# Cross-attention in a one-core float32 encoder block: a third pair of k-tiles in seven products, and the softmax's transposes queued behind the newest unit

## The chip, the cores and the metric

The kernel runs on one core of a Trainium2 chip. The metric is the time of one execution on the device in microseconds (us), and a lower time is better. A core has TensorE (PE in the profile, with its weight loads as PEld), VectorE (DVE), ScalarE (ACT), GpSimd (POOL) and SyncE (SP, which issues the loads here). Every engine takes the instructions of its own queue in the order in which they stand there, and waits on semaphores for results of the others.

## The reference

One encoder layer over 256 tokens of width 2048, in float32. The change lies in the cross-attention with 256 memory tokens and 4 heads of width 512:

```python
def mem_cross_attention(h, mem_h, w_q, w_kv, w_o):
    q = (h @ w_q).reshape(b, s, XATTN_HEADS, XATTN_HEAD_DIM)
    kv = (mem_h @ w_kv).reshape(b, mem_h.shape[1], 2, XATTN_HEADS, XATTN_HEAD_DIM)
    k, v = kv[:, :, 0], kv[:, :, 1]
    logits = jnp.einsum('bshd,bmhd->bhsm', q, k).astype(jnp.float32) * (XATTN_HEAD_DIM ** -0.5)
    p = jax.nn.softmax(logits, axis=-1).astype(v.dtype)
    o = jnp.einsum('bhsm,bmhd->bshd', p, v).reshape(b, s, D_MODEL)
    return o @ w_o
...
    x = x + 0.5 * swiglu(rms_norm(x, ffn1_norm[l]), ...)
    x = x + mixer(rms_norm(x, mix_norm[l])) @ w_out[l]
    x = x + mem_cross_attention(rms_norm(x, xattn_norm[l]), rms_norm(mem, mem_norm[l]), ...)
    x = x + 0.5 * swiglu(rms_norm(x, ffn2_norm[l]), ...)
return rms_norm(x, final_norm)
```

## The kernel before

**Splitting.** Each float32 operand is split in two parts of the matmul type `fp32r`: a high part (a cast on ScalarE) and a low part (source minus high part, on VectorE). One product a·w is three matmuls: high·high, high·low, low·high. The activations of the keys' and values' stage stand split in `xs`; the weights are split as they arrive.

**Units.** All weights come in units of 1 MB (`raw`, three buffers). For a projection in `block_s` a unit holds one pair of k-tiles (2 × 128 rows) for 1024 output columns; a block has eight units, pairs 0 to 7 in a given order, and its result is 256 tokens × 1024 columns. The class `Stream` collects units and other steps (`st.unit`, `st.op(f, after)`: f comes `after` units later) and issues them in that order. The split of a unit stands two units ahead of its products (`AHEAD`), and the split halves have three buffers (`wh`, `wl`). A plain unit (`unit_p`) takes eight products, 24 matmuls of 512 columns. Its split is one cast and one subtraction over 2048 columns.

**Seven products.** A pair that is listed in a `Sums` object is taken with seven products instead of eight (the 2×2 scheme of Strassen and Winograd), 21 matmuls (`seven`, line 507). For it VectorE makes sums of the four weight blocks (`split_seven`, line 486: one over 1024 columns, two over 512), and two parts are split: the sums (`wh`, `wl`) and three of the four raw blocks (`xh`, `xl`, lines 279 and 280). The activations' sums are made once for each pair (`Sums.make`). In the keys' and values' stage `xh` and `xl` share one tag of two buffers (`att`).

**PSUM.** `ptile` hands out four tiles of two banks each, and these four are all of PSUM. A block holds two of them for its result from its first unit to its last (`open_whole`). From its first pair of seven products to its last it holds the two others for the products that are shared among the blocks (`open_parts`). `combine` (lines 574 to 579) reads those two out into an SBUF tile `sg`, and `join` (line 589) adds the first two to it.

**Keys and values.** Two rounds, b = 0 and 1: a block for the keys of heads 2b and 2b+1, then a block for the values of these heads, then (after the second round) the output projection `w_o`. Steps that belong to the keys are placed among the units of the values' block that follows: `turn_K` (transposes of the keys, 1 unit later), `logits` (line 1319: 24 matmuls of 256 columns for each head, then maximum, scaling, exponential, reciprocal and scaling on VectorE and ScalarE), `probs` (line 1341: four transposes of the probabilities and their split `PT`, 3 units later). `values` (line 1358) comes one unit after the values' block. Each of these takes PSUM tiles from the same four. K and V of a head share two buffers (`kv`), so the split of V waits for the logits that read K.

**Order.** The list of `Stream` is the program's order. Then a scheduler places the instructions on the engines' queues: it may put an instruction ahead of earlier ones that can't be issued yet. `in_turn`, `among_weights` and `tc.issue_after` fix an order: the instruction stands behind the named one on its queue. `latest` keeps the last weight instruction of ScalarE and VectorE for it.

Of the kernel before, what the change touches and what calls it, by code (L numbers as in the profile page):

```python
# [14 lines left out]
P = 128  # L15
D = 2048
# [4 lines left out]
NB = 512  # L21
# [78 lines left out]
def build(ctx, tc, I, out):  # L100
    nc = tc.nc
    st = Stream()
# [34 lines left out]
    def ptile(name):  # L137
        return psum.tile([P, 2, NB], F32, tag="ps", name=name)
# [6 lines left out]
    def uid(s):  # L145
        cnt[0] += 1
        return f"{s}{cnt[0]}"
# [25 lines left out]
    ident = head.tile([P, P], F32, tag="ident", name="ident")  # L173
# [16 lines left out]
    xs = main.tile([P, KT, 2, S], F32R, tag="xs", name="xs")  # L190
# [64 lines left out]
    latest = {}  # L255
# [14 lines left out]
    def among_weights(f):  # L270


        scalar, vector = behind_weights(f)
        latest["vector"] = vector
        if scalar is not None:
            latest["scalar"] = scalar
# [7 lines left out]
    def split(hi, lo, src):  # L284
        high = nc.scalar.copy(hi, src)
        return high, nc.vector.tensor_tensor(out=lo, in0=src, in1=f32(hi), op=ALU.subtract)
# [70 lines left out]
    def products(ps, act, k, h, wh, wl, first, last):  # L357

        tok = slice(h * P, (h + 1) * P)
        parts = [(act[:, k, 0, tok], wh), (act[:, k, 0, tok], wl), (act[:, k, 1, tok], wh)]  # L360
        for i, (a, w) in enumerate(parts):
            nc.tensor.matmul(ps, a, w, start=first and i == 0, stop=last and i == 2)  # L362

    def block_t(srcs, act, evict, delays=(0, 0), amid=None):

# [127 lines left out]
    def seven(banks, act, sums, g, fresh, ends, weights, order):  # L493
        th, tl, rh, rl = weights
        k0, k1, lo, hi = 2 * g, 2 * g + 1, slice(0, P), slice(P, S)
        a11, a12, a22 = ([act[:, k, p, t] for p in range(2)] for k, t in ((k0, lo), (k1, lo), (k1, hi)))
        s3, n1, n4, s2 = sums.parts(g)
        table = {
            "P1": (a11, rh[:, 0], rl[:, 0]), "P3": (n4, rh[:, 1], rl[:, 1]),
            "P2": (a12, rh[:, 2], rl[:, 2]), "P5": (n1, th[:, 0], tl[:, 0]),  # L500
            "P7": (s3, th[:, 1], tl[:, 1]), "P6": (s2, th[:, 2], tl[:, 2]),
            "P4": (a22, th[:, 3], tl[:, 3]),
        }
        for n in order:
            (a, b), wh, wl = table[n]
            for j, (x, w) in enumerate(((a, wh), (a, wl), (b, wh))):
                nc.tensor.matmul(  # L507
                    banks[n], x, w, start=n in fresh and j == 0, stop=n in ends and j == 2
                )

# [115 lines left out]
    def wload(dst, w, k0, n, n0, cols=NB):  # L626
        nc.sync.dma_start(
            dst, w[k0 * P : (k0 + n) * P, n0 : n0 + cols].rearrange("(k p) n -> p k n", p=P)
        )
# [9 lines left out]
    def wwide(w, n0, k0=0, nk=KT):  # L639

        def src(k):
            def load(raw):
                raw = raw.rearrange("p (k n) -> p k n", n=2 * NB)
                if len(loaded) < 3:
                    for kk in range(2):
                        parts = (0, NB) if not loaded else (0,)
                        for c in parts:
                            n = 2 * NB // len(parts)
                            wload(raw[:, kk : kk + 1, c : c + n], w, k + kk, 1, n0 + c, n)
                else:  # L650
                    wload(raw, w, k, 2, n0, 2 * NB)
                next(first_loads, None)
                loaded.append(1)
            return load
        return [src(k0 + k) for k in range(0, nk, 2)]
# [557 lines left out]
    for b in range(2):  # L1213
        block_b(wblock(w_in, (4 + b) * NB), xs, ev_v(b))
        for i in range(2):
            h = 2 * b + i
# [16 lines left out]
    def homes(of):  # L1233
        return lambda: scope.update(shared={tag: list(of[tag]) for tag in of})
# [5 lines left out]
    xa = {}  # L1240

    def xt(name, shape, dt=F32, tag=None, bufs=1):
        t = whole_lines(scope["pool"], shape, dt, tag or name, uid(name), bufs)
        xa[name] = t
        return t
# [36 lines left out]
    w_q, w_kv, w_o = I["xattn_w_q"][0], I["xattn_w_kv"][0], I["xattn_w_o"][0]  # L1282
# [2 lines left out]
    q_sums, Q_ORDER = Sums("ye", xs, (4, 5), True, 2), ((0, 1, 2, 3, 6, 4, 5, 7),  # L1285
                                                        (0, 1, 4, 2, 5, 3, 6, 7))
    Q_SEVENS = ((4,), (4, 5))
    kv_sums, KV_ORDER = Sums("ye", xs, (0, 4), True, 2), (1, 5, 2, 0, 3, 6, 4, 7)
    held = {}

    def ev_Q(b):
# [10 lines left out]
    def turn_K(h):  # L1302
        v = rows_turned(held["K", h])
        K = xa["K", h] = xt("K", [P, 4, 2, M], F32R, tag="kv", bufs=2)
        split(K[:, :, 0, :], K[:, :, 1, :], v)

    def ev_V(b):
        def evict(j, c):
            V = xa["V", 2 * b + j] = xt("V", [P, 2, 2, XHD], F32R, tag="kv", bufs=2)
            split(V[:, :, 0, :], V[:, :, 1, :], c)  # L1310
        return evict

    def logits(h):
        ps = ptile(uid("pl"))
        for t in range(2):
            tok = slice(t * P, (t + 1) * P)
            parts = [(d, a, b) for d in range(4) for a, b in ((0, 0), (0, 1), (1, 0))]
            for i, (d, a, b) in enumerate(parts):
                nc.tensor.matmul(  # L1319
                    ps[:, t, :M], ys[:, 4 * h + d, a, tok], xa["K", h][:, d, b, :],  # L1320
                    start=i == 0, stop=i == 11,
                )
        scale = XHD ** -0.5
        nm, sm = xt("nm", [P, 2], bufs=2), xt("sm", [P, 2], bufs=2)
        nc.vector.tensor_reduce(out=nm, in_=ps[:, :, :M], axis=AX.X, op=ALU.max)
        nc.vector.tensor_scalar_mul(nm, nm, -scale)
        pr = xa["P", h] = xt("P", [P, 2, M], bufs=2)
        for t in range(2):
            nc.scalar.activation(
                pr[:, t, :], ps[:, t, :M], AF.Exp, scale=scale, bias=nm[:, t : t + 1],  # L1330
                accum_out=sm[:, t : t + 1],
            )
        nc.vector.reciprocal(out=sm, in_=sm)
        for t in range(2):
            nc.vector.tensor_scalar_mul(pr[:, t, :], pr[:, t, :], sm[:, t : t + 1])

    def probs(h):
        ps = ptile(uid("pt"))
        for mtile in range(2):
            for t in range(2):  # L1340
                nc.tensor.transpose(
                    ps[:, mtile, t * P : (t + 1) * P], xa["P", h][:, t, mtile * P : (mtile + 1) * P], ident
                )
        if h % 2 == 0:
            xt("PT", [P, D], F32R)
        PT = xa["PT", h] = xa["PT"][:, h % 2 * 4 * S : (h % 2 + 1) * 4 * S].rearrange(
            "p (m a s) -> p m a s", m=2, a=2
        )
        split(PT[:, :, 0, :], PT[:, :, 1, :], ps[:, :, :S])

    def values(h):
        for p in range(2):
            ps = ptile(uid("pv"))
            for d in range(2):
                col = slice((2 * p + d) * P, (2 * p + d + 1) * P)
                parts = [(m, a, b) for m in range(2) for a, b in ((0, 0), (0, 1), (1, 0))]
                for i, (m, a, b) in enumerate(parts):
                    nc.tensor.matmul(  # L1358
                        ps[:, d, :S], xa["V", h][:, m, a, col], xa["PT", h][:, m, b, :],
                        start=i == 0, stop=i == 5,  # L1360
                    )
            split_pair(ys, 4 * h + 2 * p, ps[:, :, :S])
# [8 lines left out]
            for c, after in enumerate((5, 7, 6, 9)):  # L1371
                st.op(lambda c=c: mem_fold(c), after)
    st.op(homes(KV_HOMES))
    for g, after in zip(kv_sums.pairs, (0, 2)):
        st.op(lambda g=g: among_weights(lambda: kv_sums.make(g)), after)
    for b in range(2):
        block_s(wwide(w_kv, b * 2 * NB), xs, kv_sums, KV_ORDER, lambda j, c, b=b: held.__setitem__(
            ("K", 2 * b + j), c))
        for j in (1, 0):
            h = 2 * b + j  # L1380
            st.op(lambda h=h: turn_K(h), 1)
        for h in (2 * b, 2 * b + 1):
            st.op(lambda h=h: logits(h), 2)
            st.op(lambda h=h: probs(h), 3)
        block_s(wwide(w_kv, D + b * 2 * NB), xs, kv_sums, KV_ORDER, ev_V(b))
        for h in (2 * b, 2 * b + 1):
            st.op(lambda h=h: values(h), 1)
    st.op(homes(OUT_HOMES))
# [210 lines left out]
def program(shapes):  # L1599
    import concourse.bacc as _bacc  # L1600

    nc = _bacc.Bacc("TRN2", target_bir_lowering=False, num_devices=1)
    args = {
        name: nc.dram_tensor(f"in_{name}", shapes[name], F32, kind="ExternalInput").ap()
        for name in _INS
    }
    out = nc.dram_tensor("out", _OUT, F32, kind="ExternalOutput").ap()
    with tile.TileContext(nc, schedule_with_timeline_sim=True) as tc, ExitStack() as ctx:
        build(ctx, tc, args, out)
    return nc  # L1610
# [10 lines left out]
```

## Time and profile before

| | us |
|---|---|
| median of 3 runs | 2083.24 (2082.97 to 2084.09) |
| the profiled execution | 2082.87 |
| its span, first to last instruction | 2081.1 |
| PE busy | 2069.6 (99% of the span) |
| PEld busy | 1727.6 (83%) |
| DVE busy | 1786.6 (86%) |
| ACT busy | 1138.7 (55%) |
| POOL busy | 98.4 (5%) |

The busy times are those of the span. In the rows of the groups a line number names the source line (a helper's where a helper issues the instruction), then come engine, operation, destination and sources, shapes and count, and behind the bar the busy time in us, the mean of one in ns, and the idle time of the engine just before them with what ended it. A row of the timeline has the start in us, the duration in us, and the instruction; brackets hold the idle time before it. Times in the timeline count from the start of the span. The keys' and values' stage lies between about 1100 and 1290 us.

### The profile page before, as it was taken

To read this page: it belongs to the slowest core of one execution; us is meant where nothing else is said; L and a number is where in the kernel's file an instruction comes from. 1 tells how busy PE (TensorE), PEld (TensorE's weight loads), DVE (VectorE), ACT (ScalarE), POOL (GpSimd) and SP (SyncE) were. 2 spreads that over 40 slices of the span, in tenths; PEclk is the share of its full clock that TensorE was granted. 3 is DMA by queue.
4 is the path that set the end of the run, shared out by engine and by line. 5 is a ranking of instruction groups with operands and counts; after the bars stand their busy time and mean duration, and the time that the engine had idled before them with its cause. 6 is when DMAs were issued, how large, how long until landed. Compare 5 with 4: busy or idle time off the path is not lost.

```text
span 2081.1 us, 24343 instructions
## 1 busy us (share of the span) xinstructions
PE 2069.6 (99%) x9660; PEld 1727.6 (83%) x9660; DVE 1786.6 (86%) x1670; ACT 1138.7 (55%) x1128; POOL 98.4 (5%) x87
## 2 busy tenths in 40 slices
PE   9999999999999999999999999999999999999998
PEld 7888888888888888888888888888888888888886
DVE  7998899989998677679788777879988999889987
ACT  7655455644654545455755444656554555545554
POOL 0000000000000000000000000000100010000001
PEclk9999999999999999999999999999999999999999
DMA  7666666566656755557655455666576665676664
GB/s 264 207 201 227 235 223 219 185 223 239 227 199 218 249 167 182 162 185 272 226 179 190 162 182 180 205 222 203 181 242 212 237 207 193 223 242 222 210 226 151
DMA packets 131178, 435.95 MB, mean 209 GB/s; under 512 B 9844, under 2 KB 13528, under 8 KB 130680
## 3 DMA queue, kind: packets, MB, share of 16 engines
q1 hardware_dynamic: 130888, 433.86, 61.9%
q8 instruction: 76, 1.25, 0.2%
q10 hardware_dynamic: 176, 0.53, 0.1%
q14 instruction: 38, 0.31, 0.0%
HBM read 417.58 MB, written 16.78 MB: 209 GB/s over the span
## 4 chain that ended last, share of the span: by engine, by line
PE 99%; DMA 0%; DVE 0%; ACT 0%; SPq 0%; DVEq 0%; issue 0%; ACTq 0%
PE pt L362 59%; PE pt L507 27%; PE pa L347 7%; PE pb L362 2%; PE ph L780 1%; PE pl L1319 1%; PE pv L1358 1%; PE px L791 1%; PE pp L1012 0%; PE pe L362 0%; DMA x<-in_x 0%; PE pa L1039 0%; PE po L1161 0%; PE tm L1267 0%; PE px L717 0%; PE pq L1148 0%
## 5 line engine op out<-in xcount | busy, mean ns | idle before, releaser
L362 PE MATMUL pt<-wh,xs 128*128 128x512 f32 x2128 | 682.4, 390 | 0.1
L453 DVE TENSOR_TENSOR wl<-raw,wh 128x2048 fp32r<-128x2048 f32 (+1 forms) x256 | 552.1, 2162 | 141.7 <-ACT wh L1579 141.3
L1579 ACT CAST wh<-raw 128x2048 fp32r<-128x2048 f32 x256 | 489.4, 1913 | 300.7 <-PE pt L362 134.5
L362 PEld LDWEIGHTS pt<-wh,xs 128*128 128x128 f32 x2128 | 398.7, 188 | 81.9 <-ACT xs L236 0.4
L362 PE MATMUL pt<-wh,ys 128*128 128x512 f32 x1472 | 463.9, 389 | 0.0
L489 ACT CAST wh<-T 128x1024 fp32r<-128x1024 f32 x236 | 248.1, 1055 | 366.7 <-DVE T L486 355.8
L362 PE MATMUL pt<-wl,xs 128*128 128x512 f32 x1064 | 414.5, 390 | 0.0
L362 PEld LDWEIGHTS pt<-wh,ys 128*128 128x128 f32 x1472 | 276.2, 188 | 56.9
L362 PE MATMUL pt<-wl,ys 128*128 128x512 f32 x736 | 286.8, 390 | 0.0
L453 DVE TENSOR_TENSOR wl<-T,wh 128x2048 fp32r<-128x2048 f32 (+1 forms) x118 | 264.7, 2243 | 0.8 <-ACT wh L489 0.4
L362 PEld LDWEIGHTS pt<-wl,xs 128*128 128x128 f32 x1064 | 199.8, 188 | 41.0
L280 DVE TENSOR_TENSOR xl<-raw,xh 128x1536 fp32r<-128x1536 f32 x118 | 206.7, 1751 | 18.9 <-ACT xh L279 18.9
L279 ACT CAST xh<-raw 128x1536 fp32r<-128x1536 f32 x118 | 174.6, 1480 | 44.0 <-PE pt L507 35.1
L486 DVE TENSOR_TENSOR T<-T,raw 128x512 f32<-128x512 f32 x236 | 162.9, 690 | 6.2
L362 PEld LDWEIGHTS pt<-wl,ys 128*128 128x128 f32 x736 | 138.2, 188 | 28.6
L486 DVE TENSOR_TENSOR T<-raw 128x1024 f32<-128x1024 f32 x118 | 143.8, 1218 | 0.5
L507 PE MATMUL pt<-wh,xs 128*128 128x512 f32 x364 | 141.8, 390 | 0.0
L457 POOL TENSOR_TENSOR wl<-raw,wh 128x768 fp32r<-128x768 f32 x40 | 74.1, 1852 | 1376.2 <-DVE wl L453 1339.2
L507 PE MATMUL pt<-xh,xs 128*128 128x512 f32 x364 | 135.8, 389 | 0.0
L347 PE MATMUL pa<-xs,wh 128*128 128x512 f32 x384 | 135.6, 397 | 0.0
L507 PE MATMUL pt<-wh,xe 128*128 128x512 f32 x320 | 124.3, 389 | 0.0
L347 PE MATMUL pa<-xs,wl 128*128 128x256 f32 x384 | 106.8, 282 | 0.0
(248 smaller groups left out, 2312.4 us busy)
## 6 DMA issues: line engine op xcount, KB each, us to landing
raw<-in_ffn_w_down SPq DMA_DIRECT2D x88, 1024.0 KB, 5.6
raw<-in_ffn_w_up SPq DMA_DIRECT2D x80, 1024.0 KB, 5.0
raw<-in_ffn_w_gate SPq DMA_DIRECT2D x77, 1024.0 KB, 5.1
raw<-in_w_in SPq DMA_DIRECT2D x32, 1024.0 KB, 5.3
raw<-in_xattn_w_kv SPq DMA_DIRECT2D x32, 1024.0 KB, 5.0
raw<-in_w_out SPq DMA_DIRECT2D x16, 1024.0 KB, 5.6
raw<-in_xattn_w_q SPq DMA_DIRECT2D x16, 1024.0 KB, 5.6
raw<-in_xattn_w_o SPq DMA_DIRECT2D x16, 1024.0 KB, 5.6
```

The source lines that it names most:

```text
L279: in_turn("scalar", lambda: nc.scalar.copy(hi, src))
L280: in_turn("vector", lambda: nc.vector.tensor_tensor(out=lo, in0=src, in1=f32(hi), op=ALU.subtract))
L347: nc.tensor.matmul(o, w, x, start=k == 0 and i == 0, stop=last and i == 1)
L362: nc.tensor.matmul(ps, a, w, start=first and i == 0, stop=last and i == 2)
L453: in_turn("vector", lambda: nc.vector.tensor_tensor(out=lo[:, :n], in0=src[:, :n], in1=f32(hi[:, :n]), op=ALU.subtract))
L457: rest = nc.gpsimd.tensor_tensor(out=lo[:, n:], in0=src[:, n:], in1=f32(hi[:, n:]), op=ALU.subtract)
L486: in_turn("vector", lambda: nc.vector.tensor_tensor(out=o, in0=a, in1=b, op=ALU.add))
L489: in_turn("scalar", lambda: nc.scalar.copy(th[:, c], t[:, c]))
L507: nc.tensor.matmul(banks[n], x, w, start=n in fresh and j == 0, stop=n in ends and j == 2)
L780: nc.tensor.transpose(v[:, i, h * P : (h + 1) * P], g[:, h, i * P : (i + 1) * P], ident)
L791: nc.tensor.transpose(v[:, j, h * P : (h + 1) * P], x[:, h, j * P : (j + 1) * P], ident)
L1579: in_turn("scalar", lambda: nc.scalar.copy(hi, raw))
```

## The change

The pairs of the keys' and values' stage that take seven products go from two (0 and 4) to three (0, 4 and 2), in all four blocks. The order of the pairs changes: the first keys' block takes 1, 5, 3, 0, 6, 4, 2, 7, and the three other blocks take 1, 0, 3, 5, 2, 6, 4, 7; before, all four took 1, 5, 2, 0, 3, 6, 4, 7. The sums of the third pair are made 4 units after the stage's begin. The four transposes of `probs` come 4 units later instead of 3, and stand behind the newest matmul of a unit on TensorE's queue, which `latest["tensor"]` now keeps.

```diff
@@ products
-            nc.tensor.matmul(ps, a, w, start=first and i == 0, stop=last and i == 2)
+            latest["tensor"] = nc.tensor.matmul(
+                ps, a, w, start=first and i == 0, stop=last and i == 2
+            )
@@ seven
-                nc.tensor.matmul(
+                latest["tensor"] = nc.tensor.matmul(
                     banks[n], x, w, start=n in fresh and j == 0, stop=n in ends and j == 2
                 )
@@ the keys' and values' stage
-    kv_sums, KV_ORDER = Sums("ye", xs, (0, 4), True, 2), (1, 5, 2, 0, 3, 6, 4, 7)
+    kv_sums = Sums("ye", xs, (0, 4, 2), True, 3)
+    KV_ORDER = ((1, 5, 3, 0, 6, 4, 2, 7), (1, 0, 3, 5, 2, 6, 4, 7))
@@ probs
-                nc.tensor.transpose(
-                    ps[:, mtile, t * P : (t + 1) * P], xa["P", h][:, t, mtile * P : (mtile + 1) * P], ident
-                )
+                with tc.issue_after(latest["tensor"].ins):
+                    nc.tensor.transpose(
+                        ps[:, mtile, t * P : (t + 1) * P],
+                        xa["P", h][:, t, mtile * P : (mtile + 1) * P], ident,
+                    )
@@ the list of steps
-    for g, after in zip(kv_sums.pairs, (0, 2)):
+    for g, after in zip(kv_sums.pairs, (0, 2, 4)):
         st.op(lambda g=g: among_weights(lambda: kv_sums.make(g)), after)
     for b in range(2):
-        block_s(wwide(w_kv, b * 2 * NB), xs, kv_sums, KV_ORDER, lambda j, c, b=b: held.__setitem__(
+        block_s(wwide(w_kv, b * 2 * NB), xs, kv_sums, KV_ORDER[b], lambda j, c, b=b: held.__setitem__(
             ("K", 2 * b + j), c))
         for j in (1, 0):
             h = 2 * b + j
             st.op(lambda h=h: turn_K(h), 1)
         for h in (2 * b, 2 * b + 1):
             st.op(lambda h=h: logits(h), 2)
-            st.op(lambda h=h: probs(h), 3)
-        block_s(wwide(w_kv, D + b * 2 * NB), xs, kv_sums, KV_ORDER, ev_V(b))
+            st.op(lambda h=h: probs(h), 4)
+        block_s(wwide(w_kv, D + b * 2 * NB), xs, kv_sums, KV_ORDER[1], ev_V(b))
         for h in (2 * b, 2 * b + 1):
             st.op(lambda h=h: values(h), 1)
```

## The prediction

> **What bounds the kernel now.** I read the chain of waits first, then the waits by engine, then the timelines of the keys' and values' stage. The page's chain, back from the last instruction, by engine:
>
> ```profile
> PE 99%; DMA 0%; DVE 0%; ACT 0%; SPq 0%; DVEq 0%; issue 0%; ACTq 0%
> ```
>
> TensorE is the bound: the chain is its own work, and the waits by engine list none for it in this stage. The chain in order of time gives the price of its work:
>
> ```profile
> 1150.74 5.63 PE pl L1319 x47
> ...
> 1180.48 14.96 PE pt L362 x66
> ```
>
> A matmul of 512 columns follows the last by 14.96 / 66 = 0.227 us, one of 256 columns (the logits) by 5.63 / 47 = 0.120 us. So time is saved only by fewer matmuls, and lost wherever TensorE's queue meets an instruction whose input is late.
>
> **Part 1: fewer matmuls.** A pair in seven products has 21 matmuls instead of 24. One more pair in each of four blocks takes away 4 × 3 = 12, and 12 × 0.227 = 2.7 us leave the path, wherever it stays unbroken. Over 0.2% of this kernel's time (4.2 us) can be told from no change; 2.7 us alone can't.
>
> **Part 2: VectorE's added work in the first keys' block.** Two pairs in seven products (4 and 2) now follow each other there, and the sums of the third pair are made between them. TensorE begins the block's first such pair here, VectorE the low half of the unit behind it here:
>
> ```profile
> 1108.97 0.39 PE L507 MATMUL pt<-xh,xs 128*128 128x512 f32 x1
> ```
>
> ```profile
> 1092.65 0.68 DVE L424 TENSOR_TENSOR j<-xs 128x512 f32<-128x512 f32 x1
> 1093.37 0.29 DVE L431 TENSOR_TENSOR j<-j 128x128 f32<-128x128 f32 x1
> ...
> 1097.89 0.29 DVE L286 TENSOR_TENSOR xs<-j,xs 128x128 fp32r<-128x128 f32 x1
> 1098.09 0.55 DVE L286 TENSOR_TENSOR ye<-j,ye 128x384 fp32r<-128x384 f32 x1
> ...
> 1110.26 2.28 DVE L453 TENSOR_TENSOR wl<-raw,wh 128x2048 fp32r<-128x2048 f32 x1
> ```
>
> The end of the first values' block has the prices of a split in seven products (1189.89 to 1196.29 without its V rows: sums 1.22 and 1.41, raw low part 1.75; then `wl`, 2.29):
>
> ```profile
> 1182.67 0.69 DVE L579 TENSOR_TENSOR sg<-pt,sg 128x512 f32<-128x512 f32 x1
> 1183.28 1.48 DVE L453 TENSOR_TENSOR wl<-raw,wh 128x1280 fp32r<-128x1280 f32 x1
> 1184.68 2.35 DVE L589 TENSOR_TENSOR sg<-pt,sg 128x1024 f32<-128x1024 f32 x2
> 1187.68 2.29 DVE L453 TENSOR_TENSOR wl<-raw,wh 128x2048 fp32r<-128x2048 f32 x1 [0.65 <-ACT wh L1579]
> 1189.89 1.22 DVE L486 TENSOR_TENSOR T<-raw 128x1024 f32<-128x1024 f32 x1
> 1191.02 2.35 DVE L286 TENSOR_TENSOR V<-sg,V 128x1024 fp32r<-128x1024 f32 x2
> 1193.29 1.41 DVE L486 TENSOR_TENSOR T<-T,raw 128x512 f32<-128x512 f32 x2
> 1194.62 1.75 DVE L280 TENSOR_TENSOR xl<-raw,xh 128x1536 fp32r<-128x1536 f32 x1
> ```
>
> Each row begins some 0.08 us before the one ahead of it ends, so steps are counted 0.08 shorter than their rows. From 1110.26 the changed queue has: a moved low part 0.21, the unit's `wl` 2.21, pair 4's sums 1.13 and 1.33 with the `ye` part 0.47 between, its `xl` 1.67 and `wl` 2.21, the new sums (0.72 and four times 0.3: 1.9), pair 2's first sum 1.13, the new low parts with the wait for their casts 1.8, then 1.33 and 1.67 for pair 2's second sums and `xl`: 17.1 us, until 1127.4. TensorE wants that `xl` after 21 + 24 + 21 + 4 = 70 matmuls from 1108.97, at 1124.9. It waits 2.5 us there, and some 0.3 around it for casts. That pushes the first values' block too: its second unit is a pair in seven products now, whose raw buffer comes free late, and its split stands ahead of the joins and of the next unit's `wl`. In the second keys' block pair 2, the fourth unit, stands behind the values' splits. At each of the two places a `wl` can come late by 0 to its own 2.29 us; I take 1.3 for both together, nearer to the low end since two units of TensorE's work lie between. Sum 2.5 + 0.3 + 1.3 = 4.1 us, between 0 (slack that I don't see) and 7.4 (both `wl` late in full).
>
> **Part 3: logits that get no PSUM until the values' block ends.** In the values' blocks pair 0 now stands second, not fourth. `open_parts` comes with it, ahead of the logits in the program (2 units later), and so the four PSUM tiles are taken: two for the result, two for the shared products until `combine` behind pair 4, the seventh unit. The order of the changed program's instructions on TensorE shows it: all eight units of the values' block, then the 48 logits matmuls of both heads, then at once the four transposes of the first head and one of the second, then the next block's first unit. Before, the logits stood among the third unit's matmuls, and further units' matmuls lay between them and the transposes. The new `issue_after` is no cover: its anchor is a matmul of the fourth unit, long past. Nor could the next unit stand ahead: its two PSUM tiles are those of the logits, free when the exponentials have read them.
>
> So TensorE waits for the softmax with nothing to do. Call T0 the end of the values' block on TensorE; before, it is the release of this cast:
>
> ```profile
> 1185.73 1.92 ACT L1579 CAST wh<-raw 128x2048 fp32r<-128x2048 f32 x1 [3.27 <-PE pt L362]
> ```
>
> `combine` ends at 1182.67 + 0.69 = T0 - 2.4. The softmax's rows in the first values' block before are:
>
> ```profile
> 1153.53 0.69 DVE L1325 TENSOR_REDUCE nm<-pl 128x2 f32<-128x512 f32 x1 [1.56 <-PE pl L1319]
> 1154.26 0.17 DVE L1326 TENSOR_SCALAR nm<-nm 128x2 f32<-128x2 f32 x1
> 1156.86 0.17 DVE L1333 RECIPROCAL sm<-sm 128x2 f32<-128x2 f32 x1 [2.43 <-ACT P L1329]
> 1157.06 0.62 DVE L1335 TENSOR_SCALAR P<-P,sm 128x256 f32<-128x256 f32 x2
> 1157.59 0.69 DVE L1325 TENSOR_REDUCE nm<-pl 128x2 f32<-128x512 f32 x1
> 1158.31 0.17 DVE L1326 TENSOR_SCALAR nm<-nm 128x2 f32<-128x2 f32 x1
> 1159.63 0.17 DVE L1333 RECIPROCAL sm<-sm 128x2 f32<-128x2 f32 x1 [1.15 <-ACT P L1329]
> ```
>
> ```profile
> 1154.51 1.28 ACT L1329 ACT_TABLE_LOAD   x1 [4.86 <-DVE nm L1326]
> ```
>
> *First round.* VectorE's queue behind `combine` in the changed program: the split of the next keys' block's second unit, now in seven products (1.22, 1.41, 1.75, 1.48 with POOL's share taken off), the two joins 2.35: 7.8 us, until T0 + 5.4. The first head's logits are done long before (T0 + 2.9). Then its maximum 0.69, a plain unit's `wl` 2.29, the second head's maximum 0.69, one V low part 1.18, the first head's scaling 0.17: T0 + 10.2. From a scaling's end to the reciprocal's start are 2.43 us with the table load, then 0.17 and half of 0.62 until the first transpose can start: T0 + 13.2. The logits end at T0 + 48 × 0.120 = T0 + 5.75, so TensorE waits 7.45 us. The second head's exponentials follow at once (T0 + 13.6, 1.03 us behind the first's), its reciprocal and first scaling at T0 + 14.15; the four transposes
>
> ```profile
> 1160.55 0.60 PE L1341 MATMUL pt<-ident,P 128*128 128x128 f32 x4
> ```
>
> fill about 0.4 of that, and 0.65 more is waited: 8.1 us.
>
> *Second round.* The next block is `w_o`, whose second unit is plain, so VectorE reaches the joins early. They end 1.3 us behind T0 before:
>
> ```profile
> 1283.36 2.35 DVE L589 TENSOR_TENSOR sg<-pt,sg 128x1024 f32<-128x1024 f32 x2
> ```
>
> ```profile
> 1284.41 1.92 ACT L1579 CAST wh<-raw 128x2048 fp32r<-128x2048 f32 x1 [3.27 <-PE pt L362]
> ```
>
> Its sums begin (0.68, 0.29), the first maximum can end at T0 + 3.6. Then 0.29, 0.17, 0.29, V 1.18, two of 0.29, a `wl` 2.29: T0 + 8.1. The exponentials, without a table load, are done by then. Reciprocal 0.17, the second maximum 0.69, the other V 1.18, `ye` 0.55, half of 0.62: transposes at T0 + 11.0, a wait of 5.25. The second head's scaling follows, 1.15 to its reciprocal, and its transpose comes at T0 + 13.1, 1.7 behind the first four: 7.0 us.
>
> Bounds for both waits together: at least the bare softmax for each round, from the second maximum's start to the first scaled P, 1153.53 to 1157.37 = 3.8, so 7.7; at most 15.1 and a cast of 1.92 (row at 1185.73) in each, 18.9. I take 15.1, the sum along the queue. What hid all this is gone: before, units lay between every two steps of this chain.
>
> **Part 4: TensorE's clock behind the waits.** The end of the trace shows what an idle TensorE does:
>
> ```profile
> 2071.59 0.39 PE L362 MATMUL pt<-wh,ys 128*128 128x512 f32 x1
> ```
>
> ```profile
> 2072.00:2073.00 1.00, 0.00 (x0) 0.00 (x0) 0.99 (x2) 0.36 (x3) 0.37 (x1) 1.00 0.40 133
> 2076.00:2077.00 1.00, 0.00 (x0) 0.00 (x0) 0.49 (x2) 0.20 (x1) 0.00 (x0) 0.97 0.58 211
> 2077.00:2078.00 1.00, 0.00 (x0) 0.00 (x0) 0.00 (x0) 0.00 (x0) 0.00 (x0) 0.50 1.04 399
> ```
>
> The granted clock (third figure from the end) falls from 1.00 to 0.50 at 2076.94, 4.96 us after the last matmul's end at 2071.98. Both waits, 7.45 and 5.25, are longer. How long the half clock stays, the start shows:
>
> ```profile
> 1.43 2.82 PE L206 MATMUL pwarm<-ident 128*128 128x128 f32 x12 [1.43 <-POOL ident masks.py:199]
> 5.18 0.60 PE L206 MATMUL pwarm<-ident 128*128 128x128 f32 x4
> ```
>
> Twelve transposes take 2.82 us, 0.23 each, twice the later pace; four at 5.18 take the 0.60 of the row at 1160.55. So the slow pace ends between 4.2 and 5.2, after 2.75 to 3.75 us of work. Half of the middle, 1.6 us, is lost behind each wait: 3.2 us, between 0 and 3.8. The Trainium skill, page "TensorE: Matmul & The Clock Gate", section "What's actually happening", says that TensorE's clock halves after at least one idle window of about 3.4 us and comes back after about as long a busy one; the trace agrees on the fall (4.96 us idle, 0.50). By its 3.4 us the estimate would be 1.7 a wait, 3.4 in all.
>
> **Sum.** -2.7 + 4.1 + 15.1 + 3.2 = +19.7. The trace is of an execution of 2082.87 us (span 2081.1), 0.4 below the median of 2083.24. On the median: 2103 us, and a span of 2100.8. Nothing outside the stage changes; the third pair's sums are made once and serve all four blocks.
>
> **The rivals.**
> 1. *Waits without the clock.* The transposes between the two parts of each wait keep the clock up, or it falls later: +16.5, 2099.7 us. For it: the second wait is only 0.3 us over the 4.96. Against: the first is far over.
> 2. *VectorE falls further behind.* After each wait its queue stands behind the second head's transposes, values' splits and joins, and the next units' `wl` come late again: 5 us more, 2108. For it: no step of its queue can pass another. Against: its row at 1187.68 waits for a cast, so there it is ahead of TensorE.
> 3. *Bare softmax.* The scheduler's order leaves other work less in the way than I count: 7.7 instead of 15.1, clock kept: +9.1, 2092.3.
> 4. *The other side: no change that can be told.* The logits' work is hidden as before, VectorE's added 4 × 4.4 us fit its idle time, and only the twelve matmuls count: -2.7, 2080.5. It decides if TensorE gets its transposes' input before it has done its 48 logits, that is if VectorE's chain ends by T0 + 5.75 instead of T0 + 13. Nothing in the queue allows it: the joins alone end at T0 + 5.4.
>
> **How the numbers follow.** Forecast 0.60, rival 1 0.15, rival 2 0.11, rival 3 0.10, rival 4 0.04. The time is that of the forecast, 2103. The range 2094 to 2109 leaves out rivals 3 and 4 and part of rival 2, and takes in parts 2 to 4 off by half. Slower by over 0.2%: 0.95; within: 0.04 (rival 4); faster by over 0.2%: 0.01, for 4.2 us are more than the twelve matmuls give.
>
> **What would show it.** Right: 12 fewer matmuls; two gaps of TensorE of 5 to 9 us, each ahead of transposes of P behind 48 logits matmuls at a values' block's end, put down to VectorE's scaling of P; a granted clock of 0.5 for some 3 us behind each; a wait for `xl` of 2 to 3 us late in the first keys' block. Wrong: no gap ahead of the transposes, or logits amid a values' block, or gaps and a clock of 1.00 throughout (rival 1).

## The result and the profile after

The changed kernel takes 2101.76 us (median of 5 runs, 2101.22 to 2102.38) against 2083.47 us (5 runs, 2082.97 to 2084.09): a ratio of 1.0088, with a 95% interval of 1.0073 to 1.0102. It is slower by 18.3 us. The profiled execution's span is 2100.0 us, 18.9 more than before. The page of the changed kernel, busy times and then the chain by engine:

```profile
PE 2074.5 (99%) x9648; PEld 1730.6 (82%) x9648; DVE 1804.6 (86%) x1693; ACT 1146.0 (55%) x1138; POOL 98.4 (5%) x87
...
PE 97%; DVE 2%; ACT 0%; DMA 0%; issue 0%; SPq 0%; DVEq 0%; ACTq 0%
```

There are 9648 matmuls, 12 fewer than before, but VectorE now stands in the chain with 2% of the span. The waits by engine (what TensorE waits for, us in total, times, longest) name the place:

```profile
PE pt L1345 <- DVE P L1338: 11.9, 3, 6.3
PE pt L509 <- DVE xl L280: 2.1, 1, 2.1
```

Line 1345 is the transposes of the probabilities P, line 1338 the scaling of P, line 509 the products of a pair in seven products. TensorE's timeline in the changed kernel, at those four waits:

```profile
1124.16 0.40 PE L509 MATMUL pt<-wh,xs 128*128 128x512 f32 x1
1126.70 0.50 PE L509 MATMUL pt<-xl,xs 128*128 128x512 f32 x1 [2.14 <-DVE xl L280]
...
1127.75 0.63 PE L509 MATMUL pt<-xh,xs 128*128 128x512 f32 x1
1128.18 0.63 PE L509 MATMUL pt<-xl,ye 128*128 128x512 f32 x1
...
1180.99 5.91 PE L1322 MATMUL pl<-K,ys 128*128 128x256 f32 x48
1193.16 1.64 PE L1345 MATMUL pt<-ident,P 128*128 128x128 f32 x5 [6.26 <-DVE P L1338]
...
1288.00 5.91 PE L1322 MATMUL pl<-K,ys 128*128 128x256 f32 x48
1298.71 1.09 PE L1345 MATMUL pt<-ident,P 128*128 128x128 f32 x4 [4.79 <-DVE P L1338]
1300.69 0.45 PE L1345 MATMUL pt<-ident,P 128*128 128x128 f32 x1 [0.89 <-DVE P L1338]
```

All 48 logits matmuls stand at the values' blocks' ends, and behind them TensorE waits for the softmax. Behind the first wait the matmuls start 0.43 us apart instead of 0.227. The stretches of the changed kernel (from:to, length, busy time of PE, PEld, DVE, ACT and POOL with counts, granted clock, DMA share, GB/s) show the clock:

```profile
1123.76:1127.17 3.41, 1.27 (x6) 0.76 (x5) 3.38 (x4) 2.41 (x3) 0.00 (x0) 1.00 0.00 0
1127.17:1130.58 3.41, 3.41 (x10) 2.63 (x9) 3.41 (x2) 2.48 (x2) 0.00 (x0) 0.50 0.80 251
...
1188.61:1192.03 3.42, 0.00 (x0) 0.00 (x0) 3.42 (x5) 1.32 (x4) 0.00 (x0) 1.00 0.37 90
1192.03:1195.44 3.41, 2.18 (x7) 1.64 (x8) 2.53 (x9) 1.98 (x7) 0.00 (x0) 0.50 0.53 217
1195.44:1198.85 3.41, 3.41 (x9) 2.64 (x8) 0.15 (x1) 0.00 (x0) 0.00 (x0) 0.50 0.00 0
1198.85:1202.27 3.42, 3.42 (x18) 2.79 (x17) 0.40 (x1) 0.59 (x1) 0.00 (x0) 1.00 0.00 0
```

The clock is halved for one stretch of 3.41 us behind the first wait and for two such stretches behind each of the two long waits. (The third halving is seen from 1297.84 to 1304.67, in the same way.)

**The balance.** I added up, for all of TensorE's matmuls in the stage, by how much the next one starts later than is usual for its form. The waits give 2.14 + 6.26 + 4.79 + 0.89 = 14.08 us. What lies above the usual pace behind them gives 1.87 in the first keys' block, 3.14 in the first round, 2.79 in the second, and 0.36 in the second keys' block. The kernel before has 0.34 of its own here. With the 12 matmuls saved: 14.08 + 8.16 - 0.34 - 2.72 = +19.2. The traces agree: from the stage's first matmul of a pair in seven products to the same matmul of `w_o` it is 218.2 us before (1108.97 to 1327.19) and 237.6 now (1108.52 to 1346.08), 19.3 more. I call this length the stage's below. The medians of all runs lie 18.3 apart; a single trace can differ from them, by its start among other things (the stage begins 0.45 later in the trace of the kernel before).

### The profile page after: what moved, and what is told of

Read it like the earlier page. It is cut to its first block, busy times and chain, and to the rows that moved or that the text cites. A ratio compares the mean times of both kernels' runs of the same rounds, so it can differ in the third digit from the quotient of the medians.

```text
span 2100.0 us, 24348 instructions
## 1 busy us (share of the span) xinstructions
PE 2074.5 (99%) x9648; PEld 1730.6 (82%) x9648; DVE 1804.6 (86%) x1693; ACT 1146.0 (55%) x1138; POOL 98.4 (5%) x87
## 4 chain that ended last, share of the span: by engine, by line
PE 97%; DVE 2%; ACT 0%; DMA 0%; issue 0%; SPq 0%; DVEq 0%; ACTq 0%
PE pt L362 57%; PE pt L509 27%; PE pa L347 6%; PE pb L362 2%; PE ph L782 1%; PE pv L1363 1%; PE px L793 0%; DVE wl L455 0%; PE pp L1014 0%; PE pe L362 0%; DMA x<-in_x 0%; DVE V L286 0%; PE pa L1041 0%; PE po L1163 0%; PE tm L1269 0%; DVE xl L280 0%
## 5 line engine op out<-in xcount | busy, mean ns | idle before, releaser
L362 PE MATMUL pt<-wh,xs 128*128 128x512 f32 x2064 | 666.2, 392 | 0.4 <-ACT xs L236 0.4
L455 DVE TENSOR_TENSOR wl<-raw,wh 128x2048 fp32r<-128x2048 f32 (+1 forms) x252 | 545.4, 2170 | 131.1 <-ACT wh L1584 130.7
L1584 ACT CAST wh<-raw 128x2048 fp32r<-128x2048 f32 x252 | 481.5, 1912 | 277.0 <-PE pt L362 122.6
L491 ACT CAST wh<-T 128x1024 fp32r<-128x1024 f32 x244 | 256.6, 1055 | 378.8 <-DVE T L488 371.2
L362 PEld LDWEIGHTS pt<-wh,xs 128*128 128x128 f32 x2064 | 388.3, 188 | 80.4 <-ACT xs L236 0.6
L362 PE MATMUL pt<-wl,xs 128*128 128x512 f32 x1032 | 403.5, 392 | 0.0
L455 DVE TENSOR_TENSOR wl<-T,wh 128x2048 fp32r<-128x2048 f32 (+1 forms) x122 | 271.5, 2225 | 0.8 <-ACT wh L491 0.4
L280 DVE TENSOR_TENSOR xl<-raw,xh 128x1536 fp32r<-128x1536 f32 x122 | 213.7, 1751 | 18.6 <-ACT xh L279 18.6
L279 ACT CAST xh<-raw 128x1536 fp32r<-128x1536 f32 x122 | 180.5, 1480 | 57.9 <-PE pt L509 45.0
L509 PE MATMUL pt<-wh,xs 128*128 128x512 f32 x380 | 148.3, 390 | 0.0
L509 PE MATMUL pt<-xh,xs 128*128 128x512 f32 x380 | 142.4, 391 | 0.0
```

The lines of the kernel that those rows point to most:

```text
L279: in_turn("scalar", lambda: nc.scalar.copy(hi, src))
L280: in_turn("vector", lambda: nc.vector.tensor_tensor(out=lo, in0=src, in1=f32(hi), op=ALU.subtract))
L362: latest["tensor"] = nc.tensor.matmul(ps, a, w, start=first and i == 0, stop=last and i == 2)
L455: in_turn("vector", lambda: nc.vector.tensor_tensor(out=lo[:, :n], in0=src[:, :n], in1=f32(hi[:, :n]), op=ALU.subtract))
L491: in_turn("scalar", lambda: nc.scalar.copy(th[:, c], t[:, c]))
L509: latest["tensor"] = nc.tensor.matmul(banks[n], x, w, start=n in fresh and j == 0, stop=n in ends and j == 2)
```

## Experiments

**Theories.** A, the prediction's: pair 0 in second place in the values' blocks takes the PSUM tiles before the logits do, so the softmax stands at the block's end with no TensorE work beside it. B: VectorE's added work for the third pair makes the softmax late. C: the transposes' new place makes the waits. All runs have the kernel before beside them, at 2083.3 to 2083.7 us.

### The transposes' place alone

```diff
-    kv_sums = Sums("ye", xs, (0, 4, 2), True, 3)
-    KV_ORDER = ((1, 5, 3, 0, 6, 4, 2, 7), (1, 0, 3, 5, 2, 6, 4, 7))
+    kv_sums = Sums("ye", xs, (0, 4), True, 2)
+    KV_ORDER = ((1, 5, 2, 0, 3, 6, 4, 7), (1, 5, 2, 0, 3, 6, 4, 7))
...
-    for g, after in zip(kv_sums.pairs, (0, 2, 4)):
+    for g, after in zip(kv_sums.pairs, (0, 2)):
```

(This is an edit of the changed kernel, like the others where nothing else is said.)

> The kernel before with one half of the change alone: probs four units late, its transposes behind the newest unit's matmul; two pairs in seven products and the old order. Theory A (the place of the first pair in seven products, second in the values' blocks, takes the PSUM tiles before the logits and so puts the softmax at the block's end): this half costs nothing. The logits stay amid the values' block's third unit, a unit and more lies between them and the transposes, no wait of TensorE ahead of the transposes; within 1.0 us of the kernel before (2082.5 to 2084.5). Theory B (VectorE's added sums and splits make the softmax late): the same, since no such work is added. Theory C (the transposes' new place on TensorE's queue makes the waits): waits of some 5 us at both rounds, 2095 or more.

Measured: 2083.06 us, ratio 0.9998 (0.9990 to 1.0007). The chain of this kernel, then its logits and the first transposes of P in TensorE's timeline:

```profile
PE 99%; DMA 0%; DVE 0%; ACT 0%; SPq 0%; DVEq 0%; issue 0%; ACTq 0%
```

```profile
1150.67 5.80 PE L1322 MATMUL pl<-K,ys 128*128 128x256 f32 x47
...
1184.44 0.60 PE L1345 MATMUL pt<-ident,P 128*128 128x128 f32 x4
```

The logits stand amid the values' block, where they were before, and TensorE waits for nothing in the stage. The transposes come late, at the block's end (1184.44, where the kernel before has them at 1160.55), but by then P is ready. Theory C falls: this half of the change costs nothing by itself.

### The pairs and the order alone

```diff
-                with tc.issue_after(latest["tensor"].ins):
-                    nc.tensor.transpose(
+                nc.tensor.transpose(
...
-            st.op(lambda h=h: probs(h), 4)
+            st.op(lambda h=h: probs(h), 3)
```

> The changed kernel with the transposes as before (3 units late, not tied to a matmul): the third pair and the new order alone. Theory A: the logits still get no PSUM until the values' block ends, so all three waits and half-clock stretches stay: 2101 to 2103, within 1 us of the changed kernel. Theory B: the same. Theory C: the two waits at the blocks' ends go, some 14 us less with the clock: 2086 to 2090.

Measured: 2101.97 us, ratio 1.0089 (1.0076 to 1.0103), the time of the changed kernel. The waits by engine of this kernel:

```profile
PE pt L1344 <- DVE P L1338: 11.9, 3, 6.2
PE pt L509 <- DVE xl L280: 2.1, 1, 2.1
```

The same waits stand there without the transposes' edit. So the whole loss comes from the pairs and their order.

### The order alone

```diff
-    kv_sums, KV_ORDER = Sums("ye", xs, (0, 4), True, 2), (1, 5, 2, 0, 3, 6, 4, 7)
+    kv_sums, KV_ORDER = Sums("ye", xs, (0, 4), True, 2), ((1, 5, 3, 0, 6, 4, 2, 7), (1, 0, 3, 5, 2, 6, 4, 7))
```

(The blocks take the two orders as in the changed kernel; this is an edit of the kernel before.)

> The kernel before with the new order of pairs alone: two pairs in seven products (0 and 4), pair 0 second in the values' blocks; no third pair, transposes as before. Theory A: logits at the end of both values' blocks, two waits for P of 5 to 7 us (some 12 together), each with a stretch of half clock behind it (some 2 to 3 us lost for each); no wait for xl in the first keys' block: +16 or so, 2097 to 2102. Theory B (the third pair's work on VectorE): within 2 us of the kernel before, 2082 to 2086. Theory C: as before too, 2083.

Measured: 2098.82 us, ratio 1.0075 (1.0059 to 1.0090). Its waits by engine:

```profile
PE pt L1341 <- DVE P L1335: 12.0, 2, 6.9
```

Without any third pair the order brings 15.1 of the 18.3 us, and the same 12 us of waits for P. Theory B falls for these two waits: the third pair's work on VectorE adds nothing to them. The third pair brings the other 3 us (4.0 by the stage's length, 233.5 us here), although it saves 2.7: the wait for `xl` with the clock behind it (2.14 + 1.87 in the balance), 0.36 in the second keys' block, and a longer half clock behind the waits for P (3.14 + 2.79 us above the usual pace in the changed kernel, 3.4 in this one).

### The values' blocks with pair 0 fourth

```diff
-        block_s(wwide(w_kv, D + b * 2 * NB), xs, kv_sums, KV_ORDER[1], ev_V(b))
+        block_s(wwide(w_kv, D + b * 2 * NB), xs, kv_sums, (1, 5, 3, 0, 6, 4, 2, 7), ev_V(b))
```

> The changed kernel with one order changed: both values' blocks take 1, 5, 3, 0, 6, 4, 2, 7 (the order of the first keys' block), so the first pair in seven products stands fourth and the logits, two units late, get their PSUM first. Three pairs, transposes as in the changed kernel. Theory A: logits amid the block again, transposes a unit and more behind them, both waits at the blocks' ends gone with their half clock; what stays is the wait for xl in the first keys' block (2.1 us) with its own half clock (1.6 to 2): -2.7 + 2.1 + 1.8 = +1.2 on the kernel before, 2083 to 2087. Theory B (VectorE's work for three pairs makes the softmax late wherever the logits stand): waits for P of 3 us or more stay, 2090 to 2100.

Measured: 2093.04 us, ratio 1.0044 (1.0032 to 1.0057). The waits for P are gone, but 8.7 us of the 18.3 are won where I expected 15 or more. The time lies in the range that I gave theory B, though not by the waits for P that it asks for. TensorE's timeline, then VectorE's:

```profile
1154.66 5.79 PE L1322 MATMUL pl<-K,ys 128*128 128x256 f32 x47
...
1188.19 1.20 PE L1345 MATMUL pt<-ident,P 128*128 128x128 f32 x8
1193.52 0.66 PE L362 MATMUL pt<-wh,xs 128*128 128x512 f32 x1 [4.13 <-DVE PT L286]
```

```profile
1191.11 1.75 DVE L280 TENSOR_TENSOR xl<-raw,xh 128x1536 fp32r<-128x1536 f32 x1
1192.78 1.28 DVE L286 TENSOR_TENSOR PT<-pt,PT 128x512 fp32r<-128x512 f32 x2
```

The logits are amid the block again, as theory A has it. But the transposes, four units late, come after `open_parts` in the program, and by the order in which the four PSUM tiles are handed out they get theirs only when `combine` has released one; they stand at the block's end. (No run has this order with the transposes three units late, which would test this reading.) The next block's first unit needs their tile, and its read-out (`PT`) stands on VectorE behind a split in seven products. A new wait of 4.13 us takes the place of the 6.26, with 3.41 us of half clock behind it. My expectation had the logits' place right and missed this wait.

### The same order in the second keys' block too

```diff
-    KV_ORDER = ((1, 5, 3, 0, 6, 4, 2, 7), (1, 0, 3, 5, 2, 6, 4, 7))
+    KV_ORDER = ((1, 5, 3, 0, 6, 4, 2, 7), (1, 5, 3, 0, 6, 4, 2, 7))
```

> The kernel of the run before (values' blocks 1, 5, 3, 0, 6, 4, 2, 7), with the second keys' block in that order too, so the unit behind the first values' block's end is a plain one. Reading of the 4.13 us wait for PT that was left there: the split in seven products of the second keys' block's second unit (T 1.21 and 1.42, xl 1.75) stands on VectorE ahead of PT's low part. If so, that wait and its half clock go: 2093.0 - 4.1 - 1.7 = 2087, and the first keys' block's wait for xl (2.1) stays, with a half clock or without: 2084 to 2088. Rival: the transposes' late place (behind the eighth unit) alone makes PT late, whatever VectorE has ahead of it: 2092 to 2094.

Measured: 2088.45 us, ratio 1.0024 (1.0015 to 1.0033), a little above the 2084 to 2088 that I had expected. TensorE's timeline at the same place:

```profile
1187.01 1.03 PE L1345 MATMUL pt<-ident,P 128*128 128x128 f32 x8
1188.34 0.50 PE L362 MATMUL pt<-wh,xs 128*128 128x512 f32 x1 [0.29 <-DVE sg L591]
```

The transposes stand as late as in the last run, and the wait is 0.29 instead of 4.13. So it was the split of the second keys' block's second unit on VectorE that made `PT` late, and not the transposes' late place alone. Left over are small waits: 2.14 for `xl` in the first keys' block; 0.19, 0.32 and 1.00 in the second keys' block; 0.29 and 0.26 at the values' blocks' ends. They are more than the 2.7 us that the matmuls save.

### Two pairs in the first keys' block

```diff
-            ("K", 2 * b + j), c))
+            ("K", 2 * b + j), c), sevens=((0, 4), None)[b])
...
-    for g, after in zip(kv_sums.pairs, (0, 2, 4)):
+    for g, after in zip(kv_sums.pairs, (0, 2, 7)):
```

(On top of the last run's order.)

> As the run with 1, 5, 3, 0, 6, 4, 2, 7 in all blocks, but the first keys' block takes only pairs 0 and 4 in seven products, and pair 2's sums are made 7 units after the stage's begin instead of 4. If the wait for xl in the first keys' block comes from two such units in a row with the new sums between them, it goes with its half clock: three matmuls more (+0.7) and 2.1 to 3.9 less than that run; 9 matmuls fewer than the kernel before, -2.0: 2081 to 2083. Rival (VectorE is too full in every block, so the wait only moves to the values' blocks): 2084 or more.

Measured: 2085.61 us, ratio 1.0010 (1.0000 to 1.0019). Its waits by engine:

```profile
PE pt L509 <- DVE xl L280: 1.2, 2, 1.0
...
PE pt L362 <- DVE sg L591: 0.5, 2, 0.3
PE pt L509 <- DVE wl L455: 0.3, 1, 0.3
```

The wait of 2.14 in the first keys' block is gone, so two units in seven products in a row with new sums between them were its cause. The smaller ones of the other blocks stay, and the kernel isn't faster than before: the time lies in the rival's range, above the 2081 to 2083 that I had expected. But the wait didn't move there; the smaller ones stood in the last run too.

### Pair 2's sums made earlier

```diff
-    for g, after in zip(kv_sums.pairs, (0, 2, 4)):
+    for g, after in zip(kv_sums.pairs, (0, 2, 2)):
```

(Three pairs in all blocks, the order 1, 5, 3, 0, 6, 4, 2, 7 in all.)

> As the run with 1, 5, 3, 0, 6, 4, 2, 7 in all blocks, three pairs everywhere, with pair 2's sums made 2 units after the stage's begin (with pair 4's) instead of 4. If it is the sums between xh and xl of pair 2 that make xl late (1.9 for the sums, about 1.1 for their low parts and casts), the wait shrinks from 2.1 to under 0.5 and no half clock follows: 12 matmuls fewer at full effect, 2080.5 to 2082. Rival: the two buffers that xh and xl of both pairs share set xl's time (the cast of pair 2's xh waits for pair 4's last product that reads them), or the sums now make pair 4 late instead: a wait of 1 us or more stays, 2083 to 2087.

Measured: 2087.78 us, ratio 1.0019 (1.0010 to 1.0028). Its waits by engine:

```profile
PE pt L362 <- DVE wl L455: 1.7, 1, 1.7
PE pt L509 <- DVE xl L280: 1.5, 3, 1.0
```

In the first keys' block the wait for `xl` falls from 2.14 to 0.32, and one of 1.66 for a plain unit's `wl` comes in its place. The time is the rival's, and so is the direction, though the new wait stands ahead of a plain unit and not of pair 4: VectorE's queue has no room there for the sums, and moving them moves the wait.

### TensorE's waits filled with spare work

```diff
         ps = ptile(uid("pt"))
+        for _ in range((36, 0, 26, 0)[h]):
+            with tc.issue_after(latest["tensor"].ins):
+                nc.tensor.transpose(ps[:, 0, :P], ident, ident)
```

> The changed kernel with spare transposes of the identity into the first head's PSUM tile, ahead of its four: 36 in the first round, 26 in the second (about 0.15 us each, 5.4 and 3.9 us). They fill TensorE's waits and change nothing that P waits for. If the half clock behind the waits costs what the balance leaves for it (about 2.5 us for each of the two), it goes and the kernel is 4 to 6 us faster than the changed one: 2096 to 2098. By the prediction's 1.6 for each: 2098.5. If the rest is something else (the refill of the pipeline, later work on VectorE): 2101 to 2103.

Measured: 2101.80 us, ratio 1.0084 (1.0070 to 1.0098), the changed kernel's time. The spare transposes took 0.113 us each, not 0.15, and left a wait of 2.23 + 0.47 in the first round. The stretches there:

```profile
1192.37:1195.79 3.42, 1.48 (x8) 1.06 (x9) 2.91 (x9) 2.42 (x9) 0.00 (x0) 1.00 0.65 253
1195.79:1199.20 3.41, 3.41 (x10) 2.64 (x9) 0.21 (x1) 0.00 (x0) 0.00 (x0) 0.50 0.00 0
```

The clock still fell, though for one stretch of 3.41 us in each round where the changed kernel has two, and in this trace not behind the wait for `xl`. Spare work and waits of the two places came to 12.9 us instead of 11.9, and the stage's length is 1.4 us shorter (236.1) but begins 1.4 later, so the run says little of the clock's price. It showed that a stretch that is 43% busy (1.48 of 3.42) is idle enough. The next kernel fills the waits wholly:

```diff
-        for _ in range((36, 0, 26, 0)[h]):
+        for _ in range((54, 0, 41, 0)[h]):
```

> As the run with spare transposes, but as many as the waits hold: 54 in the first round, 41 in the second (0.113 us each there, 6.1 and 4.6 us). With the waits filled TensorE has no window with much idle time at the values' blocks' ends. If the half clock there is set by idle time, it goes in both rounds and with it most of the 2.98 and 3.5 us that stand behind the waits in the changed kernel: 4 to 6 us less than the changed kernel, 2096 to 2098; the waits themselves stay as spare work. Rival: what stands behind the waits is not the clock: 2101 to 2102.

Measured: 2098.54 us, ratio 1.0072 (1.0056 to 1.0089). TensorE's timeline and the stretches:

```profile
1187.54 6.06 PE L1344 MATMUL pt<-ident 128*128 128x128 f32 x54
1193.86 0.81 PE L1348 MATMUL pt<-ident,P 128*128 128x128 f32 x4 [0.27 <-DVE P L1338]
```

```profile
1192.56:1195.97 3.41, 2.67 (x18) 1.98 (x17) 2.90 (x9) 2.24 (x9) 0.00 (x0) 1.00 0.59 240
1195.97:1199.39 3.42, 3.42 (x16) 2.82 (x15) 0.04 (x1) 0.00 (x0) 0.00 (x0) 1.00 0.02 5
```

The clock stays at 1.00 in both rounds, and the kernel is 3.2 us faster than the changed one, just outside the 4 to 6 that I expected (4.0 by the stage's length, 233.6; the fall behind the wait for `xl` is there in both traces). Behind the waits 0.65 and 0.62 us above the usual pace remain, where the changed kernel has 3.14 and 2.79. The half clock took 4.7 us of matmul time, then, of which 3.2 showed in the medians: part of it lay beside the wait for the second head's P, which is late anyway (0.47 and 1.26 us here, none and 0.89 in the changed kernel).

### Pairs in seven products apart from each other

```diff
-    KV_ORDER = ((1, 5, 3, 0, 6, 4, 2, 7), (1, 5, 3, 0, 6, 4, 2, 7))
+    KV_ORDER = ((1, 5, 2, 0, 3, 6, 4, 7), (1, 5, 0, 3, 4, 6, 2, 7))
```

(On top of the run with two pairs in the first keys' block.)

> The first keys' block as in the kernel before (1, 5, 2, 0, 3, 6, 4, 7, pairs 0 and 4 in seven products), the three other blocks with three pairs in the order 1, 5, 0, 3, 4, 6, 2, 7: the first of them third (the logits still come first in the program), a plain unit between any two, and a plain second unit. If the small waits of the run with two such pairs in the first block (xl 0.19 and 1.00, wl 0.29 in the second keys' block, sg 0.27 and 0.23 at the values' blocks' ends) come from units in seven products in a row, they go, and 9 matmuls fewer remain: -2.0, 2081 to 2082. Rival: VectorE's load with three pairs is what is late, wherever they stand: 2084 to 2087.

Measured: 2086.44 us, ratio 1.0015 (1.0006 to 1.0024). TensorE's timeline in the first values' block:

```profile
1161.49 0.50 PE L509 MATMUL pt<-xh,xs 128*128 128x512 f32 x1 [0.50 <-ACT P L1332]
1163.78 0.72 PE L509 MATMUL pt<-xh,xs 128*128 128x512 f32 x2 [0.63 <-ACT xh L279]
1165.57 0.50 PE L509 MATMUL pt<-xl,xs 128*128 128x512 f32 x1 [0.83 <-DVE xl L280]
```

Pair 0 as third unit takes the logits' PSUM tiles right behind them and waits for the exponential that reads them. `xh` and `xl` of the next pair wait in turn. In the second keys' and the second values' block waits of 0.2 us for `xl` stay, with 0.9 us above the usual pace in each block, although no two such units stand in a row. So spacing alone doesn't make room, though the loss in the first values' block comes from PSUM here and not from VectorE's load: in every place tried, a third pair's 0.68 us for each block were given back. No kernel with a third pair beats the one before.

## Why the prediction was right

The forecast was 2103, the measurement 2101.76; sign and mechanism held, but the sum came closer than its terms, which is luck. The terms were these.

**Part 1**, -2.7: right, 12 matmuls fewer.

**Part 2**, +4.1: the wait for `xl` measured 2.14 where 2.5 was forecast (`xl` ended at 1126.64, forecast 1127.4), and the run with two pairs in the first keys' block showed its cause as forecast. The 1.3 for late `wl`s, of which no row gave the size, didn't come: TensorE waits for no `wl` in the changed kernel, and only 0.36 us of slower pace stand in the second keys' block. That term was mis-sized.

**Part 3**, +15.1: the place, the cause and the order of events were right, and the runs with the order alone and with pair 0 fourth showed that the order of the pairs makes it. The size was 11.9. VectorE's queue in the first round of the changed kernel, with ScalarE's table load:

```profile
1178.13 0.69 DVE L581 TENSOR_TENSOR sg<-pt,sg 128x512 f32<-128x512 f32 x1
...
1184.40 2.35 DVE L591 TENSOR_TENSOR sg<-pt,sg 128x1024 f32<-128x1024 f32 x2
1186.66 0.68 DVE L1328 TENSOR_REDUCE nm<-pl 128x2 f32<-128x512 f32 x1
...
1191.19 0.16 DVE L1329 TENSOR_SCALAR nm<-nm 128x2 f32<-128x2 f32 x1
...
1192.47 0.16 DVE L1336 RECIPROCAL sm<-sm 128x2 f32<-128x2 f32 x1
1192.66 0.61 DVE L1338 TENSOR_SCALAR P<-P,sm 128x256 f32<-128x256 f32 x2
```

```profile
1188.00 1.28 ACT L1332 ACT_TABLE_LOAD   x1
```

With T0 at 1181.2 the joins end at T0 + 5.6 (forecast 5.4) and the scaling behind the second maximum and a V low part starts at T0 + 10.0 (forecast: ended by 10.2). Then the forecast had the table load on the path, 2.43 us from the scaling's end to the reciprocal. It stands here 3 us earlier, beside VectorE's work, and 1.12 are left (1191.35 to 1192.47), so the transposes start at T0 + 12.0, not 13.2, and the second head's first one follows without the 0.65 that was forecast. That is the step that was off. In the second round they start 10.5 behind T0 (1288.2), forecast 11.0 (the gap of 4.79 is just under the 5 to 9 of the forecast's signs), and the second head's transpose waits 0.89, not 1.7.

**Part 4**, +3.2: two falls were forecast, and filling those two waits saved 3.2 us. But a third fall came behind the wait of 2.14, with 1.5 us (1.87 less the 0.41 that stand around a 2.14 us wait without a fall in the run with one order in all blocks). And the half clock lasted two stretches behind each long wait, 6.83 us where some 3 were forecast, which cost 4.7 in matmul time; that 3.2 of it showed in the medians, as forecast, is luck too. The step that failed is a term put at nothing: the prediction had seen a fall behind 4.96 us of idle time, and counted no clock loss behind the 2.5 us that it had forecast for `xl`.

The forecast sum was +19.7, the stage's measured one +19.2: Part 2 was 1.6 too large (2.14 and 0.36 measured), Part 3 3.2 too large, and Part 4, with all that stands behind the waits (7.8), 4.6 too small. These errors have opposite signs, and so the sum was closer than its terms. Rival 1 (clock kept up by the transposes) is refuted by the 0.50 of the stretches, rival 2 by the missing waits for `wl`, rivals 3 and 4 by the waits' size.

## What to carry to other kernels

When a reordering brings a phase forward that takes a shared pool (PSUM here), look for who gets its tiles later than before: the logits lost their place amid the block though no line of theirs was edited, and their whole chain lost its cover. Before an engine's saved matmuls are counted, look at the queue of the engine that prepares them: with VectorE at 86% busy, each 0.68 us saved on TensorE asked 4.5 us of VectorE (its busy time rose by 18.0 over four blocks), and every place that was tried gave it back as a wait. And reckon with a clock loss behind a wait of a couple of microseconds too, not only behind the long ones: one of 2.14 us brought it in three of the six traces that have such a wait.

## What was not expected of the hardware

The granted clock falls and returns on a grid of 3.413 us: in the changed kernel at 1127.17, 1192.03 and 1297.84, which are 19 and 31 steps of 3.413 apart. What counts is how much of one grid window TensorE is idle, not how long one wait lasts. In the stage, over the traces of the twelve kernels here, every full-clock window with 1.94 us or more of idle time was followed by a half-clock one, and none with 1.79 or less. The same wait of 2.14 for `xl` shows both. In the changed kernel it lies in one window (idle 2.14, first of the stretches shown above) and the clock falls. In the run with the pairs and the order alone 1.79 of it lies in a window, and the clock stays:

```profile
1123.51:1126.92 3.41, 1.62 (x8) 0.98 (x6) 3.25 (x5) 2.41 (x4) 0.00 (x0) 1.00 0.00 0
1126.92:1130.33 3.41, 3.07 (x13) 2.35 (x14) 3.41 (x3) 3.31 (x2) 0.00 (x0) 1.00 0.58 157
```

At half clock a window with 1.24 to 1.82 us idle wasn't enough to bring the clock back, which made the half clock last 6.83 us behind both long waits; in the run with the order alone it came back after windows with 0.36 and 0.50 idle. The Trainium skill, page "TensorE: Matmul & The Clock Gate", section "What's actually happening", has the window of 3413 ns and that it runs freely; the traces agree. Its condition for the fall, at least one idle window, is too strict here: a window with 37% of TensorE's time busy (1.27 of 3.41) was followed by a fall.

A fall that isn't taken gains less than its price. In the trace of the run with the pairs and the order alone the first one is missing, and the stage's length is 0.8 us shorter than in the changed kernel (236.8), not 1.5, since part of it returns as a wait for `wl` (0.4 us, 0.8 with the pace around it) further on. The medians (2101.97 and 2101.76) hide this, for by their mean granted clock the executions of one kernel differ in it: those of these two kernels with 0.995, as in that trace, took 2101.2 to 2101.5 us, those with 0.994, as in the changed kernel's trace, 2101.8 to 2103.1.
